# A running log-sum-exp on one core: the last row pair stored as 112 partitions and four stores of four

## Chip, cores, metric

One core of a Trainium2 chip. The metric is the device time of one execution in microseconds. The kernel before takes 1250.87 us (median of three runs, 1250.59 to 1250.93). A comparison is called faster or slower from 2% on, 25 us here.

## The reference

```
x: 8 x 4096 x 2048 float32
out[:, 0] = x[:, 0]
out[:, t] = log(exp(out[:, t-1]) + exp(x[:, t]))     # with the larger one taken out first
```

It is a running log-sum-exp along the second axis.

## The kernel before

There are 64 tiles of 512 rows. Partition p holds four consecutive rows of 8 KB, so a tile is 4 MB and 32 KB a partition. SyncE loads into six buffers; ScalarE takes exp; VectorE adds the four rows of a partition; TensorE forms the sum over the partitions above and carries it to the next tile; VectorE joins; ScalarE takes Ln in place and issues the store. The end of ScalarE's program, cut:

```python
def store(n, dst, turn, h=None):
    cols = slice(0, D) if h is None else half(h)
    act.wait_ge(logs, 2 * turn + (2 if h is None else h + 1))
    act.dma_start(out=dst[:, :, cols], in_=ti[n % NI][:, :, cols]
                  ).then_inc(stored[n % NI], 16)
...
for n in range(first + 1, NT):
    up, turn = n - 1, n - 1 - first
    exp(n, 0)
    if n < NT - 1:
        exp(n, 1)
    ln(up, 0, turn)
    if n == NT - 1:
        store(up, o_v[up], turn, 0)
        exp(n, 1)
    ln(up, 1, turn)
    store(up, o_v[up], turn, 1 if n == NT - 1 else None)
for h in range(2):
    ln(NT - 1, h, NT - 1 - first)
    store(NT - 1, o_v[NT - 1], NT - 1 - first, h)
```

So tiles 62 and 63 leave as two column halves each.

The softmax here doesn't subtract the row's maximum and nothing guards it: scores larger than these inputs give would overflow.

Of the kernel before, what the change touches and what calls it, by code (L numbers as in the profile page):

```python
# [9 lines left out]
def kernel(  # L10
# [20 lines left out]
    ACT = mybir.ActivationFunctionType  # L31
    nc.scalar.preload_act_table_set("natural_log_exp_and_others")  # L32

    B, S, D = x.shape
    P = 128
    R = 4
    NBLK = S // (P * R)
    NT = B * NBLK
    FD = 512
    NI = 6  # L40
    HALF = D // 2
    assert NI % 2 == 0 and NBLK % 2 == 0 and D == 4 * FD

    pool = ctx.enter_context(tc.tile_pool(name="io", bufs=1))
# [3 lines left out]
    ti = [pool.tile([P, R, D], f32, name=f"ti{i}", tag=f"ti{i}") for i in range(NI)]  # L48
# [3 lines left out]
    o_v = out.rearrange("b (k p r) d -> (b k) p r d", p=P, r=R)  # L52

    def half(h):
        return slice(h * HALF, (h + 1) * HALF)

    def event(engine, waits, updates):

        engine.add_instruction(mybir.InstEventSemaphore(  # L59
            name=f"I-{nc.next_id()}", engine=engine.engine, ins=[], outs=[],  # L60
            sync_info=mybir.SyncInfo(
                on_wait=[mybir.SyncWait(
                    sync_type="semaphore", id=s.num, ant_name=s.name,
                    wait_mode="sem-ge-imm", wait_value=n,
                ) for s, n in waits],
                on_update=[mybir.SyncUpdate(
                    sync_type="semaphore", id=s.num, ant_name=s.name,
                    update_mode=mode, update_value=n,
                ) for s, mode, n in updates],
            ),  # L70
        ))

    def take(engine, s, n):

        event(engine, [(s, n)], [(s, "sem-sub-imm", n)])

    with tc.tile_critical():  # L77
        def sems(name, n):
            return [nc.alloc_semaphore(f"{name}{i}") for i in range(n)]

        ones, shaped, logs, top = (
            sems(s, 1)[0] for s in ("ones", "shaped", "logs", "top")
        )

        loaded, stored = sems("loaded", NI), sems("stored", NI)
# [4 lines left out]
        with nc.Block() as block:  # L90

            @block.gpsimd
            def _(g):
                g.memset(before[:], 1.0).then_inc(ones, 1)  # L94
                g.memset(last[:], 1.0).then_inc(ones, 1)  # L95
                g.wait_ge(ones, 2)

                g.affine_select(  # L98
                    out=before[:], in_=before[:], compare_op=mybir.AluOpType.is_ge, fill=0.0,
                    base=-1, pattern=[[1, P]], channel_multiplier=-1,  # L100
                ).then_inc(shaped, 1)

                g.affine_select(  # L103
                    out=last[:], in_=last[:], compare_op=mybir.AluOpType.is_ge, fill=0.0,
                    base=-(P - 1), pattern=[[0, P]], channel_multiplier=1,
                ).then_inc(shaped, 1)

            @block.sync
            def _(sp):
                def load(src, n):  # L110
                    sp.dma_start(out=ti[n][:], in_=src).then_inc(loaded[n], 16)


                sp.dma_start(out=ti[0][:, 0:2, :], in_=x_v[0][:, 0:2, :]).then_inc(top, 16)
                sp.dma_start(out=ti[0][:, 2:R, :], in_=x_v[0][:, 2:R, :]).then_inc(loaded[0], 16)
                for n in range(1, NI):
                    load(x_v[n], n)
                turns = (NT - NI) // NI
                with sp.Fori(1, turns + 1) as j:
                    for n in range(NI):  # L120
                        take(sp, stored[n], 16)
                        load(x_v[bass.ds(j * NI + n, 1)][0], n)
                for n in range((turns + 1) * NI, NT):
                    take(sp, stored[n % NI], 16)
                    load(x_v[n], n % NI)
                for n in range(NT - NI, NT):

                    take(sp, stored[n % NI], 32 if n >= NT - 2 else 16)

            @block.scalar  # L130
            def _(act):
                def exp(n, h, rows=slice(0, R)):
                    t = ti[n % NI]
                    if h == 0:
                        take(act, loaded[n % NI], 16)
                    act.activation(  # L136
                        t[:, rows, half(h)], t[:, rows, half(h)], ACT.Exp
                    ).then_inc(exps[h], 1)

                def ln(n, h, turn):  # L140
                    t = ti[n % NI]
                    act.activation(  # L142
                        t[:, :, half(h)], t[:, :, half(h)], ACT.Ln
                    )._wait_ge(carried[h], turn + 1).then_inc(logs, 1)

                def store(n, dst, turn, h=None):
                    cols = slice(0, D) if h is None else half(h)
                    act.wait_ge(logs, 2 * turn + (2 if h is None else h + 1))
                    act.dma_start(
                        out=dst[:, :, cols], in_=ti[n % NI][:, :, cols]  # L150
                    ).then_inc(stored[n % NI], 16)

                def settle(turns):
                    take(act, carried[0], turns)
                    take(act, carried[1], turns)
                    take(act, logs, 2 * turns)

                take(act, top, 16)
                act.activation(ti[0][:, 0:2, :], ti[0][:, 0:2, :], ACT.Exp)  # L159
                exp(0, 0, slice(2, R))  # L160
                exp(0, 1, slice(2, R))
                turns = (NT - 2) // NI
                with act.Fori(0, turns) as j:
                    for n in range(1, NI + 1):
                        exp(n, 0)
                        exp(n, 1)
                        ln(n - 1, 0, n - 1)
                        ln(n - 1, 1, n - 1)
                        store(n - 1, o_v[bass.ds(j * NI + (n - 1), 1)][0], n - 1)
                    settle(NI)  # L170
                first = turns * NI
                for n in range(first + 1, NT):
                    up, turn = n - 1, n - 1 - first
                    exp(n, 0)
                    if n < NT - 1:
                        exp(n, 1)
                    ln(up, 0, turn)
                    if n == NT - 1:
                        store(up, o_v[up], turn, 0)
                        exp(n, 1)  # L180
                    ln(up, 1, turn)
                    store(up, o_v[up], turn, 1 if n == NT - 1 else None)
                for h in range(2):
                    ln(NT - 1, h, NT - 1 - first)
                    store(NT - 1, o_v[NT - 1], NT - 1 - first, h)
                settle(NT - first)

            @block.tensor
            def _(pe):
# [38 lines left out]
            def _(dve):  # L228
# [10 lines left out]
                def join(n, h):  # L239
                    t = ti[n]  # L240
                    dve.tensor_add(  # L241
                        t[:, :, half(h)], t[:, :, half(h)],
                        ps[n % 2][:, half(h)].unsqueeze(1).to_broadcast([P, R, HALF]),
                    )._wait_ge(ahead[h], n + 1).then_inc(joined[h], 1)
# [45 lines left out]
```

## Time and profile before

| | before |
|---|---|
| time (median of 3) | 1250.87 us |
| span of the profiled run | 1249.0 us |
| last increment of the last store, the slow DMA engine | 1247.66 us |
| last increment of the last store, the next engine | 1245.47 us |

In the kernel before each of the 131 transfers adds sixteen to its semaphore (2096 increments in all), and the trace notes each arrival. I take each as one DMA engine that has finished: from 1245.2 on the packet records show a single row of packets, and at its end the sixteenth increment of the last store. That is how engines are told apart here. The trace also has a record of every packet (start, duration, size) but no engine number in it. Within the last 15 us I joined packets into engines by their times, since each starts within a few ns of the end of the one before; where two ends fall together a join can be wrong. The window view gives, for each stretch, the busy share of the sixteen DMA engines and the GB/s. From 1000 to 1100 us a share of 1.00 goes with 433 GB/s. The end of the kernel before in steps of 2 us (the last two numbers of a line are the share and the GB/s; the zeros and the 0.50 before them are the compute engines and the TensorE clock):

```profile
1240.00:1242.00 2.00, 0.00 (x0) 0.00 (x0) 0.00 (x0) 0.00 (x0) 0.00 (x0) 0.50 1.03 422
1242.00:1244.00 2.00, 0.00 (x0) 0.00 (x0) 0.00 (x0) 0.00 (x0) 0.00 (x0) 0.50 0.92 377
1244.00:1246.00 2.00, 0.00 (x0) 0.00 (x0) 0.00 (x0) 0.00 (x0) 0.00 (x0) 0.50 0.25 100
1246.00:1248.00 2.00, 0.00 (x0) 0.00 (x0) 0.00 (x0) 0.00 (x0) 0.00 (x0) 0.50 0.04 16
```

In each the rate over the share is 400 to 410: the engines finish at different times, but none is slowed while it works (the 4 KB packets take 159 to 178 ns from 1234 on).

### The profile page before, as it was taken

How to read it: one execution, taken by the hardware profiler on the slowest of the kernel's cores; microseconds unless marked ns; L12 is line 12 of the kernel's file. 1: busy time of each engine (PE TensorE's matmuls, PEld its weight loads, DVE VectorE, ACT ScalarE, POOL GpSimd, SP SyncE). 2: the span in 40 equal slices, each digit the busy share in tenths (PEclk: the TensorE clock that was granted, in tenths of full speed). 3: DMA queues.
4: the chain of work that ended last, by engine and by line, in shares of the span. 5: the costliest groups of instructions: out<-in, count | busy, mean ns of one | idle time of the engine just before them, and what ended most of it. 6: DMA issues, size and time to landing. Idle time of an engine off the chain costs nothing. (4 is left out here: it accounts for less than half of the span.)

```text
span 1249.0 us, 3456 instructions
## 1 busy us (share of the span) xinstructions
PE 650.8 (52%) x960; PEld 215.3 (17%) x960; DVE 1023.0 (82%) x512; ACT 907.2 (73%) x258; POOL 1.1 (0%) x8
## 2 busy tenths in 40 slices
PE   3556455554566545655455544565545564465541
PEld 1112111111112111211111111121111121111110
DVE  4999978778787787887878878778787787877873
ACT  5897866867768677686776866867768677686774
POOL 0000000000000000000000000000000000000000
PEclk9897778786887868778778786777878878678785
DMA  9999999999999999999999999999999999999998
GB/s 403 420 436 430 433 430 437 433 431 434 430 436 434 431 433 430 437 434 430 434 430 436 436 430 434 430 436 437 428 434 431 436 436 429 434 430 436 436 430 354
DMA packets 20409, 537.01 MB, mean 430 GB/s; under 512 B 2096, under 2 KB 2096, under 8 KB 4144
## 3 DMA queue, kind: packets, MB, share of 16 engines
q1 hardware_dynamic: 9360, 268.44, 49.9%
q10 hardware_dynamic: 11040, 268.44, 49.9%
q8 instruction: 7, 0.11, 0.0%
q14 instruction: 2, 0.02, 0.0%
HBM read 268.44 MB, written 268.44 MB: 430 GB/s over the span
## 5 line engine op out<-in xcount | busy, mean ns | idle before, releaser
L136 ACT ACTIVATE ti<-ti 128x4096 f32<-128x4096 f32 (+1 forms) x128 | 452.6, 3582 | 310.2 <-ACTq L59 304.2
L232 DVE TENSOR_TENSOR ti<-ti 128x1024 f32<-128x1024 f32 x384 | 464.7, 1224 | 200.0 <-ACT ti L136 191.3
L241 DVE TENSOR_TENSOR ti<-ti,ps 128x4096 f32<-128x4096 f32 x128 | 560.0, 4416 | 9.4 <-PE ps L208 9.0
L208 PE MATMUL ps<-ti,before 128*128 128x512 f32 x512 | 380.4, 895 | 342.6 <-DVE ti L232 342.1
L142 ACT ACTIVATE ti<-ti 128x4096 f32<-128x4096 f32 x128 | 455.4, 3602 | 11.5 <-PE ps L197 6.0
L197 PE MATMUL ps<-ti,last 128*128 128x512 f32 x448 | 270.6, 735 | 234.2 <-DVE ti L241 234.2
L208 PEld LDWEIGHTS ps<-ti,before 128*128 128x128 f32 x512 | 128.7, 279 | 609.0 <-DVE ti L232 500.9
L197 PEld LDWEIGHTS ps<-ti,last 128*128 128x128 f32 x448 | 86.6, 214 | 401.8 <-DVE ti L241 334.7
L159 ACT ACTIVATE ti<-ti 128x4096 f32<-128x4096 f32 x1 | 3.6, 3616 | 6.5 <-ACTq L59 6.5
L32 ACT ACT_TABLE_LOAD x1 | 1.3, 1283 | 0.8 <-PEq L274 0.8
L103 POOL TENSOR_SCALAR_AFFINE_SELECT last<-last 128x128 f32<-128x128 f32 x1 | 0.3, 296 | 0.0
L98 POOL TENSOR_SCALAR_AFFINE_SELECT before<-before 128x128 f32<-128x128 f32 x1 | 0.3, 295 | 0.1
L95 POOL MEMSET last<- 128x128 f32 x1 | 0.2, 206 | 0.0
L94 POOL MEMSET before<- 128x128 f32 x1 | 0.2, 205 | 0.5 <-SPq L77 0.5
L274 POOL MEMSET const-bfloat16-1.0<- 128x1 bf16 x1 | 0.1, 103 | 0.0
L274 POOL MEMSET const-uint8-127<- 128x1 uint8 x1 | 0.1, 103 | 0.0
L274 POOL MEMSET const-float32-0.0<- 128x1 f32 x1 | 0.1, 99 | 0.3 <-issue 0.3
L274 POOL MEMSET const-float32-1.0<- 128x1 f32 x1 | 0.1, 99 | 0.0
## 6 DMA issues: line engine op xcount, KB each, us to landing
ti<-in_x_dram SPq DMA_DIRECT2D x63, 4096.0 KB, 38.4
out_dram<-ti ACTq DMA_DIRECT2D x62, 4096.0 KB, 44.0
out_dram<-ti ACTq DMA_DIRECT2D x4, 2048.0 KB, 12.9
ti<-in_x_dram SPq DMA_DIRECT2D x2, 2048.0 KB, 9.7
```

The costliest lines, as they stand in the source:

```text
L32: nc.scalar.preload_act_table_set("natural_log_exp_and_others")
L94: g.memset(before[:], 1.0).then_inc(ones, 1)
L98: g.affine_select(out=before[:], in_=before[:], compare_op=mybir.AluOpType.is_ge, fill=0.0, base=-1, pattern=[[1, P]], channel_multiplier= ...
L103: g.affine_select(out=last[:], in_=last[:], compare_op=mybir.AluOpType.is_ge, fill=0.0, base=-(P - 1), pattern=[[0, P]], channel_multiplier=1,
L136: act.activation(t[:, rows, half(h)], t[:, rows, half(h)], ACT.Exp).then_inc(exps[h], 1)
L142: act.activation(t[:, :, half(h)], t[:, :, half(h)], ACT.Ln)._wait_ge(carried[h], turn + 1).then_inc(logs, 1)
L159: act.activation(ti[0][:, 0:2, :], ti[0][:, 0:2, :], ACT.Exp)
L197: m = pe.matmul(ps[(n + 1) % 2][:, sl], last[:], ti[n % NI][:, R - 1, sl], start=True, stop=False, skip_group_check=True,)
L208: m = pe.matmul(ps[n % 2][:, sl], before[:], ti[n % NI][:, R - 1, sl], start=n % NBLK == 0, stop=True, skip_group_check=True,)
L232: a = dve.tensor_add(t[:, r, half(h)], t[:, r - 1, half(h)], t[:, r, half(h)])
L241: dve.tensor_add(t[:, :, half(h)], t[:, :, half(h)], ps[n % 2][:, half(h)].unsqueeze(1).to_broadcast([P, R, HALF]),)._wait_ge(ahead[h], n ...
L274: nc = _bacc.Bacc("TRN2", target_bir_lowering=False, num_devices=1)
```

## The change

Its intent: tile 62 leaves whole, tile 63 as two pairs of rows (a packet is then 16 KB, one partition's two rows), and the second pair, called the last pair below, in such pieces that most engines, the slow one hopefully among them, get one packet less. Cut to its core:

```diff
+    LAST = [slice(0, 2), slice(2, R)]
+    GROUPS = [slice(0, 112)] + [slice(p, p + 4) for p in range(112, P, 4)]
...
+                def store(n, dst, done, rows=slice(0, R), groups=(slice(0, P),)):
+                    act.wait_ge(logs, done)
+                    for g in groups:
+                        act.dma_start(
+                            out=dst[g, rows, :], in_=ti[n % NI][g, rows, :]
+                        ).then_inc(stored[n % NI], 16)
...
-                    exp(n, 0)
-                    if n < NT - 1:
-                        exp(n, 1)
-                    ln(up, 0, turn)
-                    if n == NT - 1:
-                        store(up, o_v[up], turn, 0)
-                        exp(n, 1)
-                    ln(up, 1, turn)
-                    store(up, o_v[up], turn, 1 if n == NT - 1 else None)
-                for h in range(2):
-                    ln(NT - 1, h, NT - 1 - first)
-                    store(NT - 1, o_v[NT - 1], NT - 1 - first, h)
+                    for h in range(2):
+                        exp(n, h)
+                    for h in range(2):
+                        ln(n - 1, h, n - 1 - first)
+                    store(n - 1, o_v[n - 1], 2 * (n - first))
+                turn = NT - 1 - first
+                ln(NT - 1, 0, turn)
+                done = 2 * turn + 1
+                for rows in LAST:
+                    ln(NT - 1, 1, turn, rows)
+                    done += 1
+                    store(NT - 1, o_v[NT - 1], done, rows,
+                          GROUPS if rows.stop == R else (slice(0, P),))
```

SyncE's last wait counts the six stores of tile 63 accordingly.

More of the change, by code (lines that the diff above doesn't have):

```diff
@@ L126, in _ @@
                 for n in range(NT - NI, NT):
-                    take(sp, stored[n % NI], 32 if n >= NT - 2 else 16)
+                    take(sp, stored[n % NI], 16 * (len(LAST) - 1 + len(GROUPS) if n == NT - 1 else 1))
             @block.scalar
@@ L138, in exp, with ln, settle @@
                     ).then_inc(exps[h], 1)
-                def ln(n, h, turn):
+                def ln(n, h, turn, rows=slice(0, R)):
                     t = ti[n % NI]
                     act.activation(
-                        t[:, :, half(h)], t[:, :, half(h)], ACT.Ln
+                        t[:, rows, half(h)], t[:, rows, half(h)], ACT.Ln
                     )._wait_ge(carried[h], turn + 1).then_inc(logs, 1)
-                def store(n, dst, turn, h=None):
-                    cols = slice(0, D) if h is None else half(h)
-                    act.wait_ge(logs, 2 * turn + (2 if h is None else h + 1))
-                    act.dma_start(
-                        out=dst[:, :, cols], in_=ti[n % NI][:, :, cols]
-                    ).then_inc(stored[n % NI], 16)
-                def settle(turns):
+                def store(n, dst, done, rows=slice(0, R), groups=(slice(0, P),)):
[4 more added lines that the diff above has]
+                        ).then_inc(stored[n % NI], 16)
+                def settle(turns, done):
                     take(act, carried[0], turns)
                     take(act, carried[1], turns)
-                    take(act, logs, 2 * turns)
+                    take(act, logs, done)
                 take(act, top, 16)
@@ L168, in _ @@
                         ln(n - 1, 1, n - 1)
-                        store(n - 1, o_v[bass.ds(j * NI + (n - 1), 1)][0], n - 1)
-                    settle(NI)
+                        store(n - 1, o_v[bass.ds(j * NI + (n - 1), 1)][0], 2 * n)
+                    settle(NI, 2 * NI)
                 first = turns * NI
                 for n in range(first + 1, NT):
-                    up, turn = n - 1, n - 1 - first
-                    exp(n, 0)
-                    if n < NT - 1:
-                        exp(n, 1)
-                    ln(up, 0, turn)
-                    if n == NT - 1:
-                        store(up, o_v[up], turn, 0)
-                        exp(n, 1)
-                    ln(up, 1, turn)
-                    store(up, o_v[up], turn, 1 if n == NT - 1 else None)
-                for h in range(2):
-                    ln(NT - 1, h, NT - 1 - first)
-                    store(NT - 1, o_v[NT - 1], NT - 1 - first, h)
-                settle(NT - first)
+                    for h in range(2):
[11 more added lines that the diff above has]
+                          GROUPS if rows.stop == R else (slice(0, P),))
+                settle(NT - first, done)
             @block.tensor
```

## The prediction

> **What bounds the kernel now.** I read the page's sums first, then its strip of forty slices, the DMA part, the timeline of the last 50 us, windows over the same stretch, and last the semaphore records in the trace, which hold the arrival of each of the sixteen increments of every transfer.
>
> ```profile
> span 1249.0 us, 3456 instructions
> PE 650.8 (52%) x960; PEld 215.3 (17%) x960; DVE 1023.0 (82%) x512; ACT 907.2 (73%) x258; POOL 1.1 (0%) x8
> DMA  9999999999999999999999999999999999999998
> DMA packets 20409, 537.01 MB, mean 430 GB/s; under 512 B 2096, under 2 KB 2096, under 8 KB 4144
> q1 hardware_dynamic: 9360, 268.44, 49.9%
> q10 hardware_dynamic: 11040, 268.44, 49.9%
> ```
>
> No compute engine passes 82%, while the DMA strip is 9 from end to end and the two queues together fill 99.8% of sixteen engines' span. The bytes (268.44 MB in, as many out) are not changed, so only the last few microseconds can move. The last part in the timeline (start, duration, engine, line):
>
> ```profile
> 1203.27 0.35 ACTq L149 DMA_DIRECT2D out_dram<-ti  x1
> ...
> 1208.53 3.62 ACT L136 ACTIVATE ti<-ti 128x4096 f32<-128x4096 f32 x1 [5.29 <-ACTq L59]
> ...
> 1215.68 0.63 ACTq L149 DMA_DIRECT2D out_dram<-ti  x1
> 1216.36 3.62 ACT L136 ACTIVATE ti<-ti 128x4096 f32<-128x4096 f32 x1 [0.71 <-ACT ti L142]
> ...
> 1223.67 8.74 DVE L241 TENSOR_TENSOR ti<-ti,ps 128x4096 f32<-128x4096 f32 x2
> ...
> 1231.86 0.54 ACTq L149 DMA_DIRECT2D out_dram<-ti  x1
> 1232.54 3.62 ACT L142 ACTIVATE ti<-ti 128x4096 f32<-128x4096 f32 x1 [0.71 <-PEq L59]
> 1236.18 0.54 ACTq L149 DMA_DIRECT2D out_dram<-ti  x1
> ```
>
> Tile 63's load has landed at 1208.4; after that only stores run: tile 61 issued at 1203.27, tile 62 in two column halves at 1215.68 and 1223.51, tile 63 in two halves at 1231.86 and 1236.18. The windows (after the clock column: mean DMA share, GB/s) show that they follow each other without a hole:
>
> ```profile
> 1230.00:1235.00 5.00, 0.00 (x0) 0.00 (x0) 2.41 (x1) 4.29 (x2) 0.00 (x0) 0.50 1.03 424
> 1235.00:1240.00 5.00, 0.00 (x0) 0.00 (x0) 0.00 (x0) 1.15 (x1) 0.00 (x0) 0.50 1.02 420
> 1240.00:1245.00 5.00, 0.00 (x0) 0.00 (x0) 0.00 (x0) 0.00 (x0) 0.00 (x0) 0.50 0.87 355
> 1245.00:1249.00 4.00, 0.00 (x0) 0.00 (x0) 0.00 (x0) 0.00 (x0) 0.00 (x0) 0.50 0.04 14
> ```
>
> The 0.87 and then 0.04 at 355 and 14 GB/s say that the engines do not end together. The semaphore records say how. The sixteen increments of the last store arrive at 1243.71, 1243.73, 1243.74, 1244.10 and so on up to 1245.47, and the sixteenth at 1247.66: one engine is 2.19 us behind the next. It is so for each store at the end (1227.90 against 1225.59 for tile 61, 1242.73 against 1240.51 for the third half), and its lag was 0.2 us at 570 us and 1.3 us at 914 us: it loses about 0.06 us in each 19.4 us turn. So one slow DMA engine, never out of work, sets the end; from its last increment to the end of the span are 1.4 us of closing instructions. The span of 1249.0 goes with 1250.76 us for that run, and 1250.87 in the median.
>
> [...]
>
> **The change part by part.**
> *Loop.* The tick counts are only rewritten; nothing moves before tile 62's end.
> *Tile 62.* It leaves whole, after both Ln. ACT then runs exp, exp, ln, ln from 1208.53 with a pitch of 3.52 us (1208.53 to 1212.05): exp of half 1 at 1212.05 instead of 1216.36, the logarithms at 1215.6 and 1219.1, the store at 1222.7 instead of halves at 1215.68 and 1223.51. The first load's packets started 1.0 us after its issue, so first packets at about 1223.8. The engines end tile 61 at 1223.4 to 1225.3 (their increments less 0.33 us, the distance of the last data packet's end from the increment in the last store), so a few fast ones run dry for up to 0.5 us. The slow one ends it at 1227.6 and does not notice. Cost on the path: 0.
> *Tile 63.* Half 1's exp is done at 1215.7, so its three row sums end at 1219.65, the two joins (4.37 each) at 1224.0 and 1228.4, against 1232.42 before. Ln of half 0 runs 1224.2 to 1227.8, Ln of two rows of half 1 (1.90 for 128x2048, the first exps) 1228.5 to 1230.4, first pair's store at 1230.4, second Ln from about 1231.1 (0.68 from issue to next activation, as at 1231.86) to 1233, then five issues at 0.35 to 0.6 each, the last out by about 1235.5. Tile 62 keeps the engines busy to at least 1233.5 and the first pair to 1238.4. All is queued in time: the extra instructions and issues cost 0.
> *Packets.* A 4 MB store takes 9.73 us (1218.17 to 1227.90 on the slow engine), two halves in 4 KB packets 9.86 (1227.90 to 1237.82 is 9.92, 1237.82 to 1247.66 is 9.84). A row pair in 16 KB packets takes 4.89 (12.84 less 7.95, the first two loads). Gain on the slow engine: 0.15 for tile 62, 0.08 for tile 63, together 0.23; with plain row pairs its last increment would come at about 1247.43.
> *112 partitions.* The slow engine has 7 packets of 16 KB instead of 8: less by 4.89/8 = 0.61. It would end at 1246.8, 0.84 before today.
> *Four stores of four.* [...] They start tile 62 between 1223.8 and 1225.3 and need 9.73 + 4.89 + 7 x 0.611 = 18.9 to reach the small stores, at 1242.7 to 1244.2. At full rate these take 4 x 0.611 = 2.44 more: increments at 1245.5 to 1247.0, level with the slow engine. [...] The increments then come at 1247.3 to 1248.8 at best and 1252.7 to 1254.2 at worst. The fast engines are spread over 1.8 us, and the first to get ahead runs on alone, so I take the lower middle: 1250, 2.4 later than today. [...]
>
> **The rivals.**
> (a) No port conflict: end at 1246.8 to 1247.0, 0.7 to 0.8 earlier, 1250.1 us. For it: the engines do not start together[...]. [...]
> (b) Port conflict as above, my main case at some 60%: 1252 to 1256, middle 1253.3. The 112-partition store could also conflict[...]; that adds up to 2 us.
> (c) [...] it would have 11 packets, 1247.43 + 3 x 0.61 = 1249.3, 1.6 later: 1252.5. One in ten.
> (d) The queue runs dry between tiles 61 and 62 for all, because tile 62 is held back: each us of delay beyond 1227.6 would count in full. The slow engine's 1227.6 against a store issued at 1222.7 leaves nearly 4 us, so I give it little.
> (e) The shorter chain of tile 63 (4 us) shortens the run: no, it is hidden behind queued stores.
>
> **Range and chances.** 0.3 x 1250.1, 0.6 x 1253.3 and 0.1 x 1252.5 make 1252.2; I say 1252.0, since the conflict may be milder. The low end allows (a) with a little more gain, the high end a nearly lockstep (b). Two per cent are 25 us, which nothing at the end can move: 0.99 within 2%.
>
> **What would show it.** Tile 62's store issued near 1222.7, the pair near 1230.4, five issues near 1233 to 1235.5; windows at the end of the span with a share near 0.25 (four engines alone) for some us. The increments of the 112-partition store should have the slow one about 0.6 earlier than a full pair's. For (b), packets of the four small stores taking well over 0.61 us; for (a), 0.61. I am wrong in mechanism if the small stores run on more than four engines, or if the last increment belongs to the slow engine alone.

"They" in *Four stores of four* are the four engines that carry the small stores, with 7 + 4 = 11 packets instead of 8; (c) is the case that the slow engine is one of them. "Port conflict" is only a name for the case that engines slow each other down when they read neighbouring partitions at once: the trace of before, where every store has 128 partitions and sixteen increments, did not show it. The sum for the small stores came to 4.3 us at best and 9.7 at worst, behind the 1242.7 to 1244.2 at which the four engines reach them, hence the last increment at 1250 and (b)'s 1253.3. The trace supports of this only the packet of 0.611 us, four of which unhindered take 2.44; the slowdown itself was assumed. The "up to 2 us" within the 112 partitions was a guess of mine. That 112 partitions are 7 packets on each of sixteen engines was assumed from 128 / 16 = 8; the store of 112 in f2_only112 raised sixteen increments.

## The result, and the profile after

1253.94 us (median of four runs, 1253.68 to 1255.78) against 1250.78 (1250.59 to 1250.93): 3.2 us slower. The ratio is 1.0028, with a 95% interval of 1.0011 to 1.0046. Ratios here are the mean time of one kernel's fast runs over that of the other's in the same rounds, so not quite the ratio of the medians. By the 2% rule it is the same.

From the page of the changed kernel, its size, DMA counts and store issues (KB each):

```profile
span 1252.0 us, 3460 instructions
DMA packets 18745, 537.01 MB, mean 429 GB/s; under 512 B 2096, under 2 KB 2096, under 8 KB 2096
...
out_dram<-ti ACTq DMA_DIRECT2D x63, 4096.0 KB, 43.8
...
out_dram<-ti ACTq DMA_DIRECT2D x1, 2048.0 KB
out_dram<-ti ACTq DMA_DIRECT2D x1, 1792.0 KB
out_dram<-ti ACTq DMA_DIRECT2D x4, 64.0 KB
```

All packets under 512 B are semaphore increments. There are 65 loads and 69 stores; sixteen increments each would be 2144. The 2096 are 130 x 16 + 4 x 4, so each small store runs on four engines. (The kernel before also shows 2096, but as 131 transfers of sixteen.) Which four of the sixteen they are, no trace shows. The timeline shows ScalarE's end:

```profile
1223.92 0.34 ACTq L151 DMA_DIRECT2D out_dram<-ti  x1
1225.26 3.62 ACT L144 ACTIVATE ti<-ti 128x4096 f32<-128x4096 f32 x1 [1.37 <-PEq L62]
1229.60 1.91 ACT L144 ACTIVATE ti<-ti 128x2048 f32<-128x2048 f32 x1 [0.71 <-PEq L62]
1231.53 0.34 ACTq L151 DMA_DIRECT2D out_dram<-ti  x1
1231.92 1.91 ACT L144 ACTIVATE ti<-ti 128x2048 f32<-128x2048 f32 x1 [0.41 <-ACT ti L144]
1233.86 5.07 ACTq L151 DMA_DIRECT2D out_dram<-ti  x5
```

Everything is issued by 1238.9. The windows:

```profile
1240.00:1242.00 2.00, 0.00 (x0) 0.00 (x0) 0.00 (x0) 0.00 (x0) 0.00 (x0) 0.50 1.05 369
1242.00:1244.00 2.00, 0.00 (x0) 0.00 (x0) 0.00 (x0) 0.00 (x0) 0.00 (x0) 0.50 1.03 385
1244.00:1246.00 2.00, 0.00 (x0) 0.00 (x0) 0.00 (x0) 0.00 (x0) 0.00 (x0) 0.50 0.67 180
1246.00:1248.00 2.00, 0.00 (x0) 0.00 (x0) 0.00 (x0) 0.00 (x0) 0.00 (x0) 0.50 0.25 74
1248.00:1250.00 2.00, 0.00 (x0) 0.00 (x0) 0.00 (x0) 0.00 (x0) 0.00 (x0) 0.50 0.14 57
```

The engines are busy for longer than before and move less while they are: 180 over 0.67 is 269, 74 over 0.25 is 296, where the kernel before had 400. The packets of the small stores, 16 KB each, in ns, from the packet records; each column is one of the four engines, as I joined them:

```
first store    3014 2592 2405 2053     starts 1244.41 to 1245.28
second         1209  611 1360 1327
third           611  611  764  716
fourth          611  611  611  611     ends 1250.34
```

An unhindered 16 KB packet takes 611 ns. The four engines that read partitions 112 to 115 together took 3.4 to 4.9 times that, 4.1 in the mean. One comes free first, runs on alone, and the others spread out behind it. The last increment is at 1250.67, against 1247.66 before.

Four engines lagged at tile 61 in this one profile (last increments 1227.35 to 1228.90, the others by 1225.54) where the profile before has one (1227.90), so the fresh profile in f1_after was taken too.

### The profile page after: what moved, and what is told of

Read it like the earlier page. It is cut to its first block, busy times and chain, and to the rows that moved or that the text cites. A ratio compares the mean times of both kernels' runs of the same rounds, so it can differ in the third digit from the quotient of the medians.

```text
span 1252.0 us, 3460 instructions
## 1 busy us (share of the span) xinstructions
PE 646.3 (52%) x960; PEld 213.2 (17%) x960; DVE 1022.9 (82%) x512; ACT 907.1 (72%) x259; POOL 1.1 (0%) x8
## 2 busy tenths in 40 slices
DMA packets 18745, 537.01 MB, mean 429 GB/s; under 512 B 2096, under 2 KB 2096, under 8 KB 2096
## 5 line engine op out<-in xcount | busy, mean ns | idle before, releaser
L211 PE MATMUL ps<-ti,before 128*128 128x512 f32 x512 | 375.1, 882 | 342.8 <-DVE ti L235 342.4
```

The lines of the kernel that those rows point to most:

```text
L211: m = pe.matmul(ps[n % 2][:, sl], before[:], ti[n % NI][:, R - 1, sl], start=n % NBLK == 0, stop=True, skip_group_check=True,)
```

## The experiments

Twelve runs in three groups (e, f, g), each group on one chip; the three chips differ. All edits are to the changed kernel, and the diffs are cut to their core. Isolated longer executions occur in each group (1257.05 for the kernel before, 1307.25 in f4_k8, 1256.09 in g3_sbfar); no time below rests on those. The one at 1307.25 is slow and left out of f4_k8's line; the others count as fast, so they enter the ratios and widen the intervals, and I read the medians. Every ratio is "the same" by the 2% rule, so the argument rests on medians, mainly within a group, and on the packets in the traces. Medians with their range:

| run | us | range | before beside it | ratio |
|---|---|---|---|---|
| e1_pairs | 1250.49 | 1250.42 to 1250.80 | 1250.82 | 0.9992 |
| e2_strided | 1252.20 | 1251.72 to 1252.72 | 1250.82 | 1.0006 |
| e3_one16 | 1250.65 | 1250.47 to 1253.03 | 1250.82 | 1.0000 |
| e4_eights | 1256.24 | 1256.12 to 1256.73 | 1250.82 | 1.0039 |
| f1_after | 1253.95 | 1252.31 to 1259.73 | 1250.88 | 1.0028 |
| f2_only112 | 1252.42 | 1252.33 to 1252.84 | 1250.88 | 1.0011 |
| f3_cols | 1250.23 | 1250.04 to 1253.46 | 1250.88 | 0.9999 |
| f4_k8 (five fast runs) | 1253.83 | 1253.32 to 1254.55 | 1250.88 | 1.0024 |
| g1_seven | 1251.75 | 1251.61 to 1252.01 | 1250.84 | 1.0008 |
| g2_sbnear | 1253.95 | 1252.48 to 1254.30 | 1250.84 | 1.0023 |
| g3_sbfar | 1251.68 | 1251.62 to 1256.09 | 1250.84 | 1.0008 |
| g4_pairs | 1250.45 | 1250.34 to 1250.61 | 1250.84 | 0.9997 |

The theory at the start: the small stores make four engines read one group of neighbouring partitions, and there they slow each other down. The expectations call it the port theory; what lies behind it no run shows, only the packet times. The rivals: the four engines have too much to carry (11 packets instead of 8); issuing costs too much; the row pairs themselves; the memory side.

**e1_pairs: row pairs alone.**

```diff
-    GROUPS = [slice(0, 112)] + [slice(p, p + 4) for p in range(112, P, 4)]
+    GROUPS = [slice(0, P)]
```

> Row pairs alone: the last pair leaves as one store of 128 partitions. Port theory: with the small stores and the store of 112 gone, the loss is gone; last increment at about 1247.4 if tile 61's store ends at 1227.9 as in the kernel before, 1250.6 us, 0.2 under before. Rival 'the loss was there before the last pair' (in the changed kernel tile 61's store ended at 1228.9, 1.0 us later than before): then 1251.6 or more, and tile 61's last increment near 1228.9 again. Rival 'row pairs themselves are slow': near 1253.9.

1250.49, as expected. Every packet of the two pairs takes 0.61 to 0.64. Windows of this run:

```profile
1240.00:1242.00 2.00, 0.00 (x0) 0.00 (x0) 0.00 (x0) 0.00 (x0) 0.00 (x0) 0.50 0.92 393
1242.00:1244.00 2.00, 0.00 (x0) 0.00 (x0) 0.00 (x0) 0.00 (x0) 0.00 (x0) 0.50 0.96 410
1244.00:1246.00 2.00, 0.00 (x0) 0.00 (x0) 0.00 (x0) 0.00 (x0) 0.00 (x0) 0.50 0.35 147
1246.00:1248.00 2.00, 0.00 (x0) 0.00 (x0) 0.00 (x0) 0.00 (x0) 0.00 (x0) 0.50 0.04 16
```

Rate over share is 420 again (147 over 0.35), with one slow engine at the end (1247.70 against 1245.47). The whole loss is therefore in the way the last pair is cut.

**e2_strided: the small stores take every fourth partition.**

```diff
+    GROUPS = [slice(0, 112)] + [slice(112 + g, P, 4) for g in range(4)]
```

> The four small stores take every fourth partition (112, 116, 120, 124 and so on): same engines, bytes and number of stores, but each of the four engines reads another group of four neighbours. Port theory: the packets of the small stores take 0.61 us instead of 1.3 to 3.0, the end comes 2 to 3 us earlier than in the changed kernel, 1250.5 to 1252 us. Rival [...] the cost of issuing four stores: no difference, 1253.9.

The rival of 11 packets on the four engines also expected no difference. Measured: 1252.20, 1.7 less than the changed kernel (which ran on other chips: 1253.94, and 1253.95 in f1_after), with the same engines, bytes and number of issues. All sixteen packets of the small stores take 611 ns. Windows of this run:

```profile
1240.00:1242.00 2.00, 0.00 (x0) 0.00 (x0) 0.00 (x0) 0.00 (x0) 0.00 (x0) 0.50 1.14 377
1242.00:1244.00 2.00, 0.00 (x0) 0.00 (x0) 0.00 (x0) 0.00 (x0) 0.00 (x0) 0.50 0.71 270
1244.00:1246.00 2.00, 0.00 (x0) 0.00 (x0) 0.00 (x0) 0.00 (x0) 0.00 (x0) 0.50 0.35 139
1246.00:1248.00 2.00, 0.00 (x0) 0.00 (x0) 0.00 (x0) 0.00 (x0) 0.00 (x0) 0.50 0.14 57
```

From 1244 on, where the small stores run, the ratio is 397 and 407; while the store of 112 runs it is 331 and 380. So the sharing of neighbours within the small stores is real, and issuing and load alone do not explain the result. But 1.7 us over row pairs remain (e1_pairs, same chip). The profile shows where: the slow engine, still in its first pair at 1241.9 when the others are already in the store of 112, has one packet of 2658 ns and one of 1108, and ends at 1248.80. It carries no small store, so it is not one of the four that do.

**e3_one16: 112 partitions and one store of 16.**

```diff
+    GROUPS = [slice(0, 112), slice(112, P)]
```

> 112 partitions and then one store of 16[...]. Port theory: [...] up to 1.8 later than row pairs alone, plus the conflicts within the 112: 1251.3 to 1253. [...] the same as row pairs alone within 0.3.

Row pairs' time within 0.3 was expected by the rival of too many packets on the four engines; that the 16 partitions go one to each of the sixteen engines, so that each has 8 packets, was assumed.

1250.65, a miss: four of six runs at 1250.5 to 1250.7, two at 1252.7 and 1253.0. The conflict is there, with packets of up to 1724 ns and 229 over 0.78, which is 294, in this window:

```profile
1244.00:1246.00 2.00, 0.00 (x0) 0.00 (x0) 0.00 (x0) 0.00 (x0) 0.00 (x0) 0.50 0.78 229
```

But in the profiled run, one of the four short ones, it hits engines that have 2.2 us to spare, and the slow engine's packets are not stretched (last increment 1247.34). I had forgotten that spare time when I put a price on the conflict. A result near row pairs does not speak against the theory. The two longer runs have no trace; that the slow engine was hit there is read from their times alone.

**e4_eights: 96 partitions and eight stores of four.**

```diff
+    GROUPS = [slice(0, 96)] + [slice(p, p + 4) for p in range(96, P, 4)]
```

> 96 partitions and eight stores of four neighbours[...]. Rival of load alone: 3 packets of 0.61 more than in the changed kernel, 1.8 us, 1255.8. Port theory: [...] 5.5 to 9 later, 1259 to 1263.

With 96 / 16 = 6 packets of the store of 96 each, the four engines have 6 + 8 = 14 here, by estimate. The 5.5 to 9 were a sum over the four further groups.

1256.24, only 2.3 over the changed kernel and near what load alone gives (1255.8). My price per group was wrong: once the four engines are spread out, as in the table of packets above, they follow each other from group to group, and a further group costs little more than its 0.61. The small packets that start after 1247.9 take 611 to 873 ns. In this run the conflict is paid at the beginning of the row of such stores, not in each.

**f1_after: the changed kernel again.** No edit.

> The changed kernel again, beside the others of this group: 1253.5 to 1254.5 (1253.94 before). In its first trace four engines instead of one lagged at tile 61 (last increment 1228.9); if that was chance, one lags here (1227.9) and the time stays, since the engines that carried the small stores were not the lagging ones.

1253.95. One engine lags at tile 61 (1228.11, the next 1226.09), so the several laggards of the first profile were of that run. The small stores' first packets take 1.68 to 2.09 us, the last ends at 1250.62; the slow engine's packets are not stretched and end at 1246.49. So in this kernel it is the small stores that end last.

**f2_only112: the small stores left out** (wrong: 16 partitions of the last pair are never written).

```diff
+    GROUPS = [slice(0, 112)]
```

> The small stores are left out, so 16 partitions of the last row pair are never written: a wrong result on purpose. Theory 'the store of 112 conflicts with itself and hits the slow engine in some runs': between 1249.9 (7 packets instead of 8 on the slow engine, 0.6 less than row pairs' 1250.49) and 1252, with packets of 0.7 to 3 us. Rival 'all the loss sits in the small stores': 1249.9 in every run, packets of 0.61.

1252.42, and all five runs between 1252.33 and 1252.84: fewer bytes than row pairs, and 1.9 slower. In the windows of this run the rate over the share is 332 and 350:

```profile
1240.00:1242.00 2.00, 0.00 (x0) 0.00 (x0) 0.00 (x0) 0.00 (x0) 0.00 (x0) 0.50 1.06 352
1242.00:1244.00 2.00, 0.00 (x0) 0.00 (x0) 0.00 (x0) 0.00 (x0) 0.00 (x0) 0.50 0.68 238
```

The slow engine's packets of the first pair include one of 1326 ns and one of 2559, 2.7 us more than two plain ones, and it ends at 1249.0. This is e2_strided's end without any small store, so the store of 112 has a cost of its own. (One run is traced; that the others were hit too is read from their times.)

**f3_cols: the same bytes per engine without the cut in partitions** (wrong too). The last pair is 128 partitions and 7/8 of the columns.

```diff
+    GROUPS = [slice(0, P)]
+                    cols = slice(0, D - 256) if groups is GROUPS else slice(0, D)
-                            out=dst[g, rows, :], in_=ti[n % NI][g, rows, :]
+                            out=dst[g, rows, cols], in_=ti[n % NI][g, rows, cols]
```

> The same bytes per engine as 112 partitions, but taken as 7/8 of the columns of all 128 partitions (a wrong result on purpose too, the last 256 columns of the last pair are never written). If 112 conflicts[...], this one has none: no packet stretched, 1249.9 to 1250.0, and all runs within 0.4.

That each engine's share of the 112 is a run of seven neighbours was a guess. Measured: 1250.23, with one run at 1253.46, so "all runs within 0.4" was a miss; that run has no trace. In the traced run no packet of the pairs is stretched (326 GB/s over a share of 0.78 from 1242 to 1244, which is 418), and the slow engine's last pair takes 4.26 us (1243.10 to 1247.36) where row pairs take 4.85 (1242.85 to 1247.70). The relief of 0.6 us is real. In the median 0.26 of it shows against row pairs, which ran on another chip. f2 less f3, on one chip, is 2.2 us: that is the price of cutting at 112 partitions. It is not the packet size, since e1_pairs has the same 16 KB packets unstretched.

**f4_k8: 96 partitions and four stores of eight, every fourth partition.**

```diff
+    GROUPS = [slice(0, 96)] + [slice(96 + c, P, 4) for c in range(4)]
```

> 96 partitions, then four stores of eight partitions, each taking every fourth[...]. Port theory: no conflict among the small stores, packets of 0.61[...]. [...] 1249.5 to 1251.5, the spread from conflicts within the 96. [...] 2 x 0.61 later than row pairs, 1251.7 or more. A correct result, and a candidate for beating both.

The first range is for a slow engine that carries none of the stores of eight, the second for one that carries them (10 packets instead of 8).

1253.83 in the five fast runs, the bad branch. The small packets take 611 ns, as the theory has it. The slow engine is among those that carry four of them: it has 10 packets after its first pair and ends last, at 1249.86. In f1_after, on the same chip, it carried none of the stores of four (it ends at 1246.49, they at 1250.62). It would have ended near 1248.2 (1242.11 + 10 x 0.611), so I estimate that conflicts in the store of 96 took some 1.6 more.

**g1_seven: a correct candidate.** Row 2 whole, row 3 without its last 512 columns, and those as 119, 7 and 2 partitions.

```diff
+    CUT = D - 512
+    GROUPS = [(slice(0, P), 2, slice(0, D)), (slice(0, P), 3, slice(0, CUT))] + [
+        (slice(a, b), 3, slice(CUT, D)) for a, b in ((0, 119), (119, 126), (126, P))]
...
+                    for g, r, c in groups or [(slice(0, P), rows, slice(0, D))]:
+                        act.dma_start(out=dst[g, r, c], in_=ti[n % NI][g, r, c]
```

> Row pair 3 leaves as row 2 of all 128 partitions, row 3 without its last 512 columns of all 128, and those 512 columns as stores of 119, 7 and 2 partitions, which go on 7, 7 and 2 engines[...]. Every engine has 14 KB a partition less conflict-free[...]. [...] its last part is 0.61 us shorter than with row pairs: 1249.9 to 1250.1, with 130 transfers of sixteen increments and three of 7, 7 and 2. [...] it has 0.6 + 1.4 us instead: 1251 or more. [...]

The first range is for a slow engine that carries none of the 2 KB packets, the second for one that does.

1251.75, again the bad branch. The page has 2112 packets under 512 B, which is 131 x 16 + 7 + 7 + 2 (131 full transfers; I had counted 130), which fits stores on 7, 7 and 2 engines. The slow engine carries seventeen of the 2 KB packets, from 1246.5 to 1247.9, and ends last: 119 / 7 = 17, so it is one of the seven.

**g2_sbnear and g3_sbfar: which side conflicts?** The small stores read neighbours and write to every fourth place, or the other way about (misplaced; 24 rows of 32,768 land wrong, which the comparison's tolerance let pass).

```diff
+    GROUPS = [(slice(0, 112), slice(0, 112))] + [
+        (slice(112 + g, P, 4), slice(112 + 4 * g, 116 + 4 * g)) for g in range(4)]   # g2; g3 has the two swapped
-                    for g in groups:
-                            out=dst[g, rows, :], in_=ti[n % NI][g, rows, :]
+                    for d, g in groups:
+                            out=dst[d, rows, :], in_=ti[n % NI][g, rows, :]
```

> A wrong result on purpose: the four small stores read four neighbouring partitions as in the changed kernel, but write to every fourth place in memory. Port theory: the reading side decides, as the changed kernel, 1253.4 to 1254.5. Rival 'neighbouring places in memory (32 KB apart) conflict': 1252.2, as with every fourth partition on both sides.

> The other way about, a wrong result on purpose: the small stores read every fourth partition and write to neighbouring places. Port theory: 1252.2, small packets of 0.61. Memory rival: 1253.4 to 1254.5, packets of 1 to 3 us.

1253.95 and 1251.68 on one chip (1252.48 to 1254.30 against 1251.62 to 1252.35, without g3_sbfar's one run at 1256.09). The first small packets take 1.70 to 2.11 us in g2_sbnear; all sixteen take 611 ns in g3_sbfar. Reading neighbours costs, wherever they are written; writing to neighbouring places showed no cost. Windows of g2_sbnear, then of g3_sbfar:

```profile
1244.00:1246.00 2.00, 0.00 (x0) 0.00 (x0) 0.00 (x0) 0.00 (x0) 0.00 (x0) 0.50 0.47 147
1246.00:1248.00 2.00, 0.00 (x0) 0.00 (x0) 0.00 (x0) 0.00 (x0) 0.00 (x0) 0.50 0.16 49
```

```profile
1248.00:1250.00 2.00, 0.00 (x0) 0.00 (x0) 0.00 (x0) 0.00 (x0) 0.00 (x0) 0.50 0.25 107
```

In g2 the ratio is 313 and 306; in g3, where besides the small stores only the late engines run, 428. (The profiled run of g3 is its slowest, 1256.09, with two engines behind from tile 61 on; its small packets are read here, not its end.)

**g4_pairs: row pairs again**, the edit of e1_pairs.

> Row pairs alone once more, beside the store on seven engines: 1250.4 to 1250.6, all packets of the last pair 0.61. If seven engines help, they are 0.4 to 0.6 under this.

1250.45, as expected. In both groups the median of row pairs lies 0.3 to 0.4 us under the kernel before (in group e 1250.42 to 1250.80 against 1250.67 to 1251.12, without that kernel's one run at 1257.05; in group g 1250.34 to 1250.61 against 1250.70 to 1251.27), but the intervals of both ratios (0.9977 to 1.0008; 0.9983 to 1.001) hold 1. By its median it is the best correct kernel here, by a hair, and g1_seven did not beat it.

## Why the prediction was right, point by point

The predicted time was 1252.0, and the main case (b) had 1252 to 1256 with 1253.3 in the middle; measured 1253.94. The main case came true; the 1252.0, an average with cases that did not, is 1.9 too low. That (b)'s middle lies within 0.7 is in part luck: the small stores began later than predicted (1244.4 to 1245.3 instead of 1242.7 to 1244.2) and then took less time (5.9 us instead of some 7, 1242.7 to 1250 less the 0.33 from a last packet to its increment), and the two errors nearly cancel.

- *The slow engine sets the end before, and the chain of tile 63 is hidden.* Right: e1_pairs shortens the chain as the change does and gains 0.3 in the median, near what the larger packets were sized at (0.23), though no gain at all also lies within both ratio intervals.
- *The queue runs dry between tiles 61 and 62, (d).* It did for the fast engines: at 1224.6 the packet records have 10 of 16 engines at work, and those that stopped waited for up to 1.3 us, not the 0.5 predicted. The slow engine did not wait, and e1_pairs, where at 1225.0 only 6 were at work, is no slower than the kernel before. The cost on the path was rightly put at 0.
- *ScalarE's timetable.* Tile 62's store was put at 1222.7 and came at 1223.92, the first pair at 1230.4 and came at 1231.53: both late by the 1.2 us by which the last load was late in this run (exp of tile 63 at 1209.76 instead of 1208.53). The five issues were put at 0.35 to 0.6 us each; a four-partition issue takes 0.9 to 1.4, against 0.34 to 0.35 for the stores of 128 and 112 partitions before them (e3_one16's store of 16 partitions, also issued right behind another, took 1.26; the cause is open). Mis-sized without effect, since the last is out at 1238.9 and the engines come to the small stores at 1244.4.
- *112 on sixteen engines, four on four.* Right by the counts: the 2096 increments for the small stores, and sixteen for the store of 112 in f2_only112.
- *The slow engine saves 0.61.* Right as a term (4.26 for the last pair in f3_cols against 4.85), but in the changed kernel it does not decide: the engines with the small stores end last.
- *Four stores of four: between 4.3 and 9.7 us*. Right: 5.9 (1244.41 to 1250.34), last increment 1250.67, predicted 1250. That it is the reading of neighbouring partitions is shown by e2_strided and by g2 against g3. What the prediction did not see is that the conflict ends once the engines are spread; e4_eights, where I priced each group alike, shows it.
- *Conflicts within the 112, "up to 2 us".* I put them into the main case as an aside. They are half of the mechanism. f2_only112 has 2.2 us over f3_cols, and there they fall on the slow engine; that this is because it reads its own partitions late, among engines that are already elsewhere, fits the times of its two stretched packets but is argued, not shown. In the changed kernel they also delay the four engines' arrival (1244.2 at the latest by the packet count, from 1239.9, where the last of the twelve engines that were not behind ends its first pair, plus 7 x 0.611; 1244.4 to 1245.3 measured).
- *The slow engine is itself one of the four, (c).* It is not: in e2_strided and f1_after it carries no small store and ends at 1248.80 and 1246.49.

The steps in order: row pairs 1250.5; a packet less on each engine without conflict 1250.2; the same by cutting at 112 partitions 1252.4; with four strided stores on four engines 1252.2; with neighbours instead 1253.95. They come from two chips, so differences under 0.3 mean nothing.

Open: why the store of 112 hits the slow engine in every run of f2_only112, in two of six of e3_one16 (both by their times), and not in the profile of f1_after. In the profiles of the hit ones (e2, f2) the first of the fast engines came to the last pair about 1.4 us earlier than in f1_after. The traces show what goes with it, the issue of tile 62's store; here e2_strided, f2_only112 and f1_after, one line each:

```profile
1222.59 0.34 ACTq L151 DMA_DIRECT2D out_dram<-ti  x1
1222.68 0.34 ACTq L151 DMA_DIRECT2D out_dram<-ti  x1
1224.10 0.34 ACTq L151 DMA_DIRECT2D out_dram<-ti  x1
```

In the hit ones it is in time for the fast engines, which go on from tile 61 one after the other. In those not hit (also the changed kernel at 1223.92, e3_one16 at 1223.86, g2_sbnear at 1223.93) only 8 to 10 of 16 engines are at work at 1224.6, and the waiting ones begin tile 62, and later the last pair, nearly together. The store's time follows that of the last load. This is a pattern in six profiles; no run set that time on purpose, and g3_sbfar (1225.16, two engines far behind, both slowed in their first pair) does not fit it. Which partitions of the 112 each engine takes was not shown, and whether its conflict too is on the reading side was not tested.

## What to carry to other kernels

When all sixteen DMA engines are the bound, count packets per engine, but also ask which partitions the engines read at the same moment: a cut that leaves 128 partitions whole (by rows or columns) kept every packet at full rate (0.61 to 0.64 us for 16 KB in e1_pairs, none stretched in f3_cols), and a cut by partitions did not (up to 2.56 in f2_only112, 3.01 in the changed kernel). A lagging engine has two faces: its lag (2.2 us in the kernel before) hides what happens on the others, and what is done to relieve it must not run into its own late packets (2.7 us more for two of them in f2_only112). Compare the GB/s with the busy share in the window view; where the quotient fell here (from 400 and more to 269 and 296), packets were stretched.

A better version would keep 128 partitions whole and give the rest to the four engines of the small stores alone; by f3_cols I estimate that it could win 0.6 us at most (the four extra packets' worth on each of these engines, 4 x 0.611 = 2.44 us, is about what the slow engine's lag hides, 2.31 us at tile 61 of the kernel before and 2.19 at its last store).
